# Parameter steps handed out at 1.0 a tile step, S5 input tiles mixed among the RWKV pairs' tiles, and three scratch pools moved

## The chip, the cores and the metric

The kernel runs on one core of a Trainium2 chip. Its time is the device time of one execution in microseconds (us). Three runs of the kernel before gave 2048.62, 2050.24 and 2052.57 us, so its median is 2050.24 us. A lower time is better.

## The reference, cut to what matters

The reference is one layer of a diffusion backbone for 256 latent tokens with 256 context tokens ahead of them. The part around the change is the token mixer:

```python
p = einsum('btd,dn->btn', h, w_in)              # one projection feeds both mixers
q = p[..., :RWKV_IN]; u = p[..., RWKV_IN:]      # RWKV-7 part, S5 part
# RWKV-7: 16 heads x 64, two directions, a scan of matrix states over the tokens
s = s * w_t - (s @ kk_t) b_t + v_t k_t;  y = s @ r_t
# S5: 64 groups x 16 channels, 64 complex states a group, two directions
lam, bb = zoh(a, log_step, b)                   # depends on weights alone
bu = bb @ u;  state = scan(lam, bu);  y5 = c @ state
o = concat([norm(y) * gate, glu(gelu(y5 + d*u))]);  x = x + gt * (o @ w_out)
```

Behind it stands a gated feed-forward part, whose weights are most of what the kernel reads. The modulation vectors (shift, scale and gate of each sub-layer) are products of silu(c) with a weight of 2048 x 12288.

## The kernel before

**Stages.** The projection runs in tiles of 128 output columns, each with 16 blocks of 128 rows as fp32r matmuls (three a block, line L430). A *pair* is two RWKV heads: three tiles (k, v, r), then a preparation of some 36 steps (`prep`, `factors`, `products`) that writes the pair's factors to HBM (`own`). After every second pair a triangular solve (`solve`, mostly POOL) gives a block `pt`. The chains (`chain`, four in all, run two at a time by `chains(0)` and `chains(1)`) then walk over eight chunks each, and load `own` and `pt` back. S5 needs its input `u` from eight tiles of its own (`s5_projected`), and it needs tables that depend on weights alone.

**Parameter steps.** These tables and some modulation blocks are made in a generator of 84 steps, called `mods` here: `early` (20 steps, five modulation blocks, L374 and L379), `s5_factors` (32 steps, tiles `MP`, `mt`, `MB`, L1319 to L1328) and `s5_toeplitz` (32 steps, tiles `C`, `mck`, `MCk`, `ks`, L1170 to L1204). The three follow one another. In `s5_toeplitz` the tiles have one buffer each: the next `C` is loaded when the last one's readers are done, and the next `MCk` is written when the last one has left for HBM.

**Who hands out the order.** `beside` walks over the tiles' steps. To each tile step it adds two or three steps of `prepare`, and 0.72 steps of `mods` on average. When `prepare` ends, `switch` closes the pools of that phase, opens those of the chains, and goes on with `chains(0)` (two steps to a tile step). Counting the generators' steps from the code: `mods` is handed out to its end at tile step 117, the switch comes at step 123, and at that point six of the eight S5 tiles are still to come. After the tiles, `s5` and `rwkv` (rest of `chains(0)`, then `chains(1)` with the outputs of the first two, `post`) are woven step by step, with seven more modulation blocks (`late`) at every twelfth step, from the pool `mw`.

**How an order becomes queues.** A planner makes one queue for each engine and one for SP, which issues all DMAs. It simulates the program, and of the instructions that are ready in its simulation it takes the one handed out earliest. (`urgent` with an offset puts a generator far ahead; with offset 0, as for `prepare` and `chains`, its instructions count as handed out at the same place as the tile step beside them.) An instruction is ready when its inputs are there and its tile has a free buffer. Each engine then runs its queue strictly in that order.

**Room.** Scratch pools are two stacks, one from the left end of each partition's memory and one from the right end. A pool opened in the room of a closed one waits for that one's last user. From the tile sizes in the code, in bytes of a partition: left: constants 19,040, `pp` (scratch of `early` and `s5_factors`) 12,288, `rp` (of the preparation) 59,392; after the switch `yp` 4,096 and `rl0` (of `chains(0)`) 65,536, so that `rl0` ends at 88,672; later `mp` (of `post`) 14,336 and `rl1` (of `chains(1)`) 65,536, so that `rl1` ends at 103,008. Right: `hp` (the projection's input) 65,536, `wp` (its weights, and `u`) 15,360, `rs` (of the solves) 29,696, `tp` (of `s5_factors`' and `s5_toeplitz`' tables) 8,704, so that `tp` lies from 110,592 to 119,296 from the right end. All four stay open until the tiles and `mods` are done; then come `mw` 12,288, `ul` 8,192, `U2` and `Z` 49,408, `sc` 7,168, `si` 16,384. PSUM has a right pool `w`=2, `d`=1 banks (tiles; `mods`), which is closed before S5's `s`=2, `d`=1 opens.

Of the kernel before, what the change touches and what calls it, by code (L numbers as in the profile page):

```python
# [10 lines left out]
F32 = mybir.dt.float32  # L11
# [7 lines left out]
NP, NF = 8, 44  # L19
# [106 lines left out]
def run(gen):  # L126

    while True:
        try:
            next(gen)  # L130
        except StopIteration as e:
            return e.value


def chained(gens):
    for g in gens:
        yield from g


def woven(a, b, na, nb):  # L140

    ia = ib = 0
    left = [a, b]
    while left:
        g = left[0] if len(left) == 1 else (a if ia * nb <= ib * na else b)
        if next(g, left) is left:
            left.remove(g)
            continue
        if g is a:
            ia += 1  # L150
        else:
            ib += 1
        yield


class Body:
# [834 lines left out]
            yield  # L991
        yield from fill

    def beside(self, tiles, prep, mods, switch, rates=(5, 9), every=0.72):


        n, rate = 0, rates[0]
        for stage in tiles:
            n += 1
            for _ in range(rate // 2 + n % 2 * (rate % 2)):  # L1000
                if next(prep, self) is self:
                    prep, mods, rate = switch(mods)
            for _ in range(int(n * every) - int((n - 1) * every)):
                next(mods, None)
        return mods
# [348 lines left out]
    def s5_scan(self, pool, half):  # L1354

        V = self.nc.vector if half else self.nc.gpsimd
        gs = slice(16 * half, 16 * half + 16)
        Z = self.Z[:, :, :, gs]
        A, I = self.AR[:, 0, :, :, gs], self.AI[:, 0, :, :, gs]
        pair = lambda n: Z[:, 1 + n:129 - n:127 - 2 * n]  # L1360
        for n in range(32, 63):
            a = pool.tile([128, 2, 2, 16], F32, tag="sa%d" % half, name="sa")
            b = pool.tile([128, 2, 2, 16], F32, tag="sb%d" % half, name="sb")
            V.tensor_tensor(out=a, in0=pair(n - 1), in1=A, op=ALU.mult)
            V.tensor_tensor(out=b, in0=pair(n - 1)[:, :, ::-1], in1=I, op=ALU.mult)
            V.tensor_tensor(out=a, in0=a, in1=pair(n), op=ALU.add)
            V.tensor_tensor(out=pair(n), in0=a, in1=b, op=ALU.add)
            if n % 2:
                yield
# [205 lines left out]
def body(tc, A, out):  # L1575
    with ExitStack() as ctx:
        b = Body(ctx, tc, A, out)
        nc = tc.nc
        b.gelu = None
        b.od, b.Y, b.q, b.ud, b.last, b.done, b.os = {}, {}, {}, {}, None, 0, None  # L1580
        b.uld = tc.dram_tile([8, 128, 256], F32, name="uld")
        left, right = (lambda st, name, bufs=1: st.enter_context(tc.tile_pool(name=name, bufs=bufs, side="left")),
                       lambda st, name, bufs=1: st.enter_context(tc.tile_pool(name=name, bufs=bufs, side="right")))

        hx, lx, mx, sx, sb, p0, pl, pr, pm, wx, ex = (ExitStack() for _ in range(11))
        b.lx = lx
        hp = right(hx, "hp")
        b.wp = right(hx, "wp", 2)
        b.pp = left(ex, "pp", 6)
        p0.enter_context(b.psum("left", t=5, v=1, m=1, y=1))  # L1590
        first = [(0, 0), (1, 0), (3, 0), (4, 0), (5, 256)]
        parts = [(6, 2), (7, 2), (9, 2), (10, 2), (12, 2), (13, 2)]
        b.parts = {}
        with tc.tile_pool(name="sp0", bufs=1, side="left") as sp0:
            ps = b.start(hp, [(i, lo, "t") for i, lo in first], parts, lambda: b.s5_params(sp0))
        b.rp = left(lx, "rp")
        b.lora(*ps[0:2])
        for (p, j), x in zip(((0, 0), (0, 1), (0, 2)), ps[2:]):
            run(b.projected(p, j, x))
        p0.close()  # L1600

        pr.enter_context(b.psum("right", w=2, d=1))
        pl.enter_context(b.psum("left", l=1, g=2, m=2))
        b.rs = right(hx, "rs")
        tiles = []
        for p in range(1, NP):
            tiles += [b.projected(p, j) for j in range(3)]
        tiles.append(b.gates())
        tiles += [b.s5_projected(jj, b.wp) for jj in range(8)]
        tp = right(hx, "tp")  # L1610
        early = chained(b.mod_steps(blk, 4 * blk, b.pp, "d", 1, "d", 6, "pp") for blk in range(8, 13))
        prep = b.urgent(b.prepare(), 0)
        first = []

        def switch(mods):
            run(early)
            lx.close()
            ex.close()
            pl.close()
            pm.enter_context(b.psum("left", m=1))  # L1620
            pl.enter_context(b.psum("left", c=2, y=2))
            b.yp = left(mx, "yp")
            first.append(b.chains(0))
            return first[0], woven(b.urgent(b.solving), mods, 44, 16), 4

        rest = b.beside(chained(tiles), prep, chained([early, b.s5_factors(b.pp, tp), b.s5_toeplitz(tp)]), switch)
        run(rest)
        hx.close()
        pr.close()

        pr.enter_context(b.psum("right", s=2, d=1))
        mw = right(wx, "mw")
        spu, spb = right(sx, "spu"), right(sb, "spb")
        with tc.high_priority(100000):
            b.s5_begin(spb, spu)
        late = chained(b.mod_steps(blk, 4 * blk, mw, "d", 2, "d", 3) for blk in range(13, 20))
        run(b.paced(woven(b.rwkv(first[0], lx, mx, pl), b.s5(sx, sb), 140, 100), late, 12))
        wx.close()

        b.x = right(ctx, "xp").tile([128, 16, 256], F32, name="x")  # L1640
        fw = right(ctx, "fw", 2)
        with tc.tile_pool(name="om", bufs=2, side="right") as om:
            b.ffn_scales(om)
            run(b.mixed(om, fw, b.x, b.x1, 0, b.os))
            for st in (lx, mx, pl, pm, pr):
                st.close()
            ctx.enter_context(b.psum("left", w=4, m=3, d=1))
            b.ffn_input(left(ctx, "h2p"), om, fw)

        b.ffn(left(ctx, "fp"), fw, chained(b.mod_steps(blk, 4 * blk, fw, "d", 2, "d", 2) for blk in range(20, 24)))  # L1650
# [15 lines left out]
```

## Time and profile before

| | us |
|---|---|
| median of three runs | 2050.24 |
| the profiled execution's own time | 2047.77 |
| its span, first to last instruction | 2046.0 |
| PE busy (TensorE matmul) | 1857.8 (91%) |
| DVE busy (VectorE) | 1272.2 (62%) |
| ACT busy (ScalarE) | 894.4 (44%) |
| POOL busy (GpSimd) | 336.9 (16%) |

All times of rows are counted from the span's start. Busy time is the time in which at least one instruction of the engine ran; a busy PE is not PE at its peak, since its matmuls overlap and their ends are modelled. PEclk is the granted TensorE clock as a share of 2.4 GHz. In a timeline, the bracket at a line's end tells how long the engine had been idle before it, and what it then waited for.

### The profile page before, as it was taken

How to read it: one execution, taken by the hardware profiler on the slowest of the kernel's cores; microseconds unless marked ns; L12 is line 12 of the kernel's file. 1: busy time of each engine (PE TensorE's matmuls, PEld its weight loads, DVE VectorE, ACT ScalarE, POOL GpSimd, SP SyncE). 2: the span in 40 equal slices, each digit the busy share in tenths (PEclk: the TensorE clock that was granted, in tenths of full speed). 3: DMA queues.
4: the chain of work that ended last, by engine and by line, in shares of the span. 5: the costliest groups of instructions: out<-in, count | busy, mean ns of one | idle time of the engine just before them, and what ended most of it. 6: DMA issues, size and time to landing. Idle time of an engine off the chain costs nothing.

```text
span 2046.0 us, 35653 instructions
## 1 busy us (share of the span) xinstructions
PE 1857.8 (91%) x13704; PEld 1446.0 (71%) x13704; DVE 1272.2 (62%) x2400; ACT 894.4 (44%) x1617; POOL 336.9 (16%) x517
## 2 busy tenths in 40 slices
PE   3899989999989799746899989999999999999997
PEld 1557766677867668524566667888888888888886
DVE  7525877559799465443865667766666566645544
ACT  2234654435646534212223444555555455544442
POOL 0300034074183471121800000000000000000000
PEclk8899988778889899857799999999999999999998
DMA  8882576525435867839879764566666665566664
GB/s 322 306 304 91 185 249 232 200 86 174 135 112 175 257 206 233 283 117 308 299 269 338 266 214 156 193 220 216 222 214 223 224 207 183 183 186 185 186 188 136
DMA packets 181147, 433.80 MB, mean 212 GB/s; under 512 B 27248, under 2 KB 59376, under 8 KB 178160
## 3 DMA queue, kind: packets, MB, share of 16 engines
q1 hardware_dynamic: 180976, 431.52, 63.5%
q8 instruction: 108, 1.77, 0.4%
q14 instruction: 63, 0.52, 0.1%
HBM read 373.12 MB, written 62.52 MB: 213 GB/s over the span
## 4 chain that ended last, share of the span: by engine, by line
PE 53%; DMA 6%; DVE 4%; POOL 2%; issue 1%; ACT 1%; SPq 0%; DVEq 0%; ACTq 0%; POOLq 0%
PE ps_w L230 28%; PE ps_m L230 12%; PE ps_w L430 3%; PE ps_d L379 2%; DMA modw<-modw_in 2%; PE ps_s L230 1%; DMA mcd<-MCk 1%; PE ps_c L841 1%; PE ps_s L1404 1%; DMA own<-own 1%; DMA MB<-mbd 1%; DMA C<-s5c_in 1%; PE ps_d L1195 1%; POOL tmp L716 0%; POOL TM L718 0%
## 5 line engine op out<-in xcount | busy, mean ns | idle before, releaser
L220 DVE TENSOR_TENSOR lo<-raw,hi 128x1024 fp32r<-128x1024 f32 (+1 forms) x327 | 371.1, 1136 | 239.0 <-ACT hi L219 235.1
L219 ACT ACTIVATE hi<-raw 128x1024 fp32r<-128x1024 f32 (+1 forms) x327 | 322.3, 987 | 285.2 <-PE ps_w L230 207.9
L230 PE MATMUL ps_m<-h,hi 128*128 128x512 f32 x688 | 247.2, 398 | 2.3 <-ACT hi L219 2.3
L230 PE MATMUL ps_w<-h,hi 128*128 128x512 f32 x688 | 248.7, 400 | 0.6 <-DVE h L1516 0.6
L230 PE MATMUL ps_w<-hid,hi 128*128 128x512 f32 x704 | 247.6, 398 | 0.0
L230 PE MATMUL ps_w<-hid,lo 128*128 128x256 f32 x704 | 195.1, 281 | 0.0
L230 PE MATMUL ps_m<-h,lo 128*128 128x256 f32 x688 | 187.2, 282 | 1.2 <-DVE lo L220 1.2
L230 PE MATMUL ps_w<-h,lo 128*128 128x256 f32 x688 | 186.5, 281 | 0.3 <-DVE lo L220 0.3
L430 PE MATMUL ps_w<-hhi,lo 128*128 128x512 f32 (+2 forms) x448 | 174.8, 390 | 7.8 <-DVE lo L214 7.8
L430 PE MATMUL ps_w<-hhi,hi 128*128 128x512 f32 (+2 forms) x448 | 175.1, 391 | 1.1 <-ACT hi L213 1.1
L430 PE MATMUL ps_w<-hlo,hi 128*128 128x512 f32 (+2 forms) x448 | 171.2, 382 | 0.0
L214 DVE TENSOR_TENSOR lo<-raw,hi 128x512 fp32r<-128x512 f32 (+1 forms) x144 | 110.0, 767 | 97.4 <-ACT hi L213 94.8
L213 ACT ACTIVATE hi<-raw 128x512 fp32r<-128x512 f32 (+1 forms) x144 | 88.9, 620 | 181.4 <-PE ps_w L430 68.3
L230 PEld LDWEIGHTS ps_w<-h,hi 128*128 128x128 f32 x688 | 129.2, 188 | 41.2 <-ACT up L238 10.9
L230 PEld LDWEIGHTS ps_w<-hid,hi 128*128 128x128 f32 x704 | 131.3, 188 | 31.4
L230 PEld LDWEIGHTS ps_m<-h,hi 128*128 128x128 f32 x688 | 129.4, 188 | 30.3 <-ACT hi L219 3.0
L230 PEld LDWEIGHTS ps_w<-hid,lo 128*128 128x128 f32 x704 | 133.0, 189 | 1.5
L230 PEld LDWEIGHTS ps_m<-h,lo 128*128 128x128 f32 x688 | 129.9, 189 | 5.6 <-DVE lo L220 1.8
L230 PEld LDWEIGHTS ps_w<-h,lo 128*128 128x128 f32 x688 | 129.9, 189 | 3.6 <-DVE lo L220 0.7
L430 PEld LDWEIGHTS ps_w<-hhi,lo 128*128 128x128 f32 (+1 forms) x448 | 91.0, 203 | 34.5 <-DVE lo L214 15.1
L430 PEld LDWEIGHTS ps_w<-hhi,hi 128*128 128x128 f32 (+1 forms) x448 | 91.3, 204 | 26.4 <-ACT hi L213 6.8
L430 PEld LDWEIGHTS ps_w<-hlo,hi 128*128 128x128 f32 (+1 forms) x448 | 91.7, 205 | 15.4 <-issue 3.1
(387 smaller groups left out, 3464.2 us busy)
## 6 DMA issues: line engine op xcount, KB each, us to landing
raw<-wup_in SPq DMA_DIRECT2D x176, 512.0 KB
modw<-modw_in SPq DMA_DIRECT2D x152, 512.0 KB
raw<-wdn_in SPq DMA_DIRECT2D x80, 512.0 KB
raw<-win_in SPq DMA_DIRECT2D x140, 256.0 KB
own<-own SPq DMA_DIRECT2D x32, 1024.0 KB
modw<-modw_in SPq DMA_DIRECT2D x80, 256.0 KB
own<-own SPq DMA_DIRECT2D x32, 640.0 KB
raw<-wout_in SPq DMA_DIRECT2D x38, 256.0 KB
```

Source lines behind the costliest of these rows:

```text
L213: nc.scalar.activation(out=hi, in_=raw, func=AF.Copy)
L214: nc.vector.tensor_tensor(out=lo, in0=raw, in1=hi.bitcast(F32), op=ALU.subtract)
L219: nc.scalar.activation(out=hi, in_=src, func=AF.Copy)
L220: nc.vector.tensor_tensor(out=lo, in0=src, in1=hi.bitcast(F32), op=ALU.subtract)
L230: mm = self.nc.tensor.matmul(out, lhsT=a, rhs=b, start=(n == 0), stop=(n == last), skip_group_check=True)
L379: self.behind(nc.tensor.matmul(ps[32 * j:32 * j + 32, :], lhsT=self.silu[:, k], rhs=ws[j], start=(k < 4), stop=(k >= 12)))
L430: self.nc.tensor.matmul(out, lhsT=w[:, j], rhs=x[:, k, lo:T], start=(k == 4 * job["qs"][0] and n == 0), stop=(k == 4 * job["qs"][1] - 1 an ...
L841: nc.tensor.matmul(U[q:q + 64, i], lhsT=pt[q:q + 64, :, 8 * i + n], rhs=Ws[q:q + 64, i], start=True, stop=True)
L1195: nc.tensor.matmul(ps[32 * g:32 * g + 32, o:o + 128], lhsT=Bd[:, 2 * g + d, i].rearrange("p a h -> p (a h)"), rhs=m, start=(i == 0 and d = ...
L1404: nc.tensor.matmul(outs[q], lhsT=X, rhs=m[:, ::-1] if d else m, start=False, stop=(d == 1 and i == 1))
```

## The change

`beside` hands out 1.0 steps of `mods` to a tile step in place of 0.72. By the same count `mods` is then handed out to its end at tile step 84, and the switch comes at step 123 as before. Each pair's three tiles are followed by one S5 tile, the eighth S5 tile and the gates' tile come last, and no tile is left at the switch. `tp` is closed at the switch, after all of `mods` has been handed out; `hp`, `wp` and `rs` are closed after the tiles as before. `mw` is opened at the switch, on the left, under `yp` and `rl0`, so that `rl0` ends at 35,424 + 65,536 = 100,960 and `rl1` at 115,296. On the right, `ul` is then first, and `ul`, `U2`, `Z`, `sc` and `si` end at 80,128, inside the 80,896 of `hp` and `wp`; two scratch tiles of `s5_scan` get one buffer in place of two for this.

```diff
-    def beside(self, tiles, prep, mods, switch, rates=(5, 9), every=0.72):
+    def beside(self, tiles, prep, mods, switch, rates=(5, 9), every=1.0):
...
-            a = pool.tile([128, 2, 2, 16], F32, tag="sa%d" % half, name="sa")
-            b = pool.tile([128, 2, 2, 16], F32, tag="sb%d" % half, name="sb")
+            a = pool.tile([128, 2, 2, 16], F32, tag="sa%d" % half, name="sa", bufs=1)
+            b = pool.tile([128, 2, 2, 16], F32, tag="sb%d" % half, name="sb", bufs=1)
...
         for p in range(1, NP):
-            tiles += [b.projected(p, j) for j in range(3)]
-        tiles.append(b.gates())
-        tiles += [b.s5_projected(jj, b.wp) for jj in range(8)]
-        tp = right(hx, "tp")
+            tiles += [b.projected(p, j) for j in range(3)] + [b.s5_projected(p - 1, b.wp)]
+        tiles += [b.s5_projected(NP - 1, b.wp), b.gates()]
+        tp = right(tx, "tp")
...
         def switch(mods):
-            run(early)
-            lx.close()
-            ex.close()
-            pl.close()
+            run(mods)
+            for st in (tx, lx, ex, pl):
+                st.close()
             pm.enter_context(b.psum("left", m=1))
             pl.enter_context(b.psum("left", c=2, y=2))
+            wide.append(left(wx, "mw"))
             b.yp = left(mx, "yp")
             first.append(b.chains(0))
-            return first[0], woven(b.urgent(b.solving), mods, 44, 16), 4
+            return first[0], b.urgent(b.solving), 4
...
-        mw = right(wx, "mw")
+        mw = wide[0]
...
-        wx.close()
...
-            for st in (lx, mx, pl, pm, pr):
+            for st in (lx, mx, wx, pl, pm, pr):
                 st.close()
```

## Rows read from the trace of the kernel before

**Rows 1.** The page: busy tenths, granted clock and DMA share in 40 slices.
```profile
PE   3899989999989799746899989999999999999997
DVE  7525877559799465443865667766666566645544
POOL 0300034074183471121800000000000000000000
PEclk8899988778889899857799999999999999999998
DMA  8882576525435867839879764566666665566664
```

**Rows 2.** Windows by stage: span, busy PE, PEld, DVE, ACT, POOL, clock, DMA.
```profile
205.00:690.00 485.00, 452.86 (x3431) 343.27 (x3430) 372.35 (x664) 260.02 (x553) 178.83 (x241) 0.86 0.52 176
690.00:852.00 162.00, 146.26 (x1763) 115.48 (x1761) 86.52 (x154) 62.91 (x143) 72.31 (x88) 0.93 0.75 238
852.00:941.00 89.00, 38.21 (x338) 24.24 (x338) 27.60 (x56) 11.22 (x28) 16.40 (x14) 0.62 0.60 186
941.00:1054.00 113.00, 97.62 (x1536) 72.73 (x1535) 81.08 (x275) 32.36 (x84) 51.69 (x136) 0.86 0.84 292
1054.00:1254.00 200.00, 188.60 (x1426) 132.63 (x1426) 128.08 (x266) 84.65 (x146) 0.00 (x0) 0.96 0.74 263
1254.00:2046.00 792.00, 774.03 (x4400) 657.35 (x4400) 467.39 (x650) 377.55 (x544) 0.00 (x0) 0.99 0.62 196
```

**Rows 3.** Tiles MP and MCk: the table steps' DVE instructions, first and last start.
```profile
L1319 DVE TENSOR_TENSOR MP<-bs,Ls x32: 664/684/1598, 397.1 to 670.6; 128x512 f32<-128x512 f32 x32
...
L1181 DVE TENSOR_TENSOR MCk<-C,Ls x32: 718/759/1769, 676.4 to 913.2; 128x576 f32<-128x576 f32 x32
```

**Rows 4.** Windows of tile MCk: busy PE (8 instructions a step), PEld, DVE, then clock.
```profile
676.00:745.00 69.00, 6.51 (x72) 3.71 (x72) 16.61 (x18) 0.90 0.75 232
745.00:852.00 107.00, 9.32 (x104) 5.06 (x104) 20.01 (x26) 0.95 0.73 240
852.00:917.00 65.00, 10.84 (x80) 5.73 (x80) 16.31 (x20) 0.59 0.50 169
```

**Rows 5.** Waits in 852 to 917: us in total, times, longest.
```profile
POOL mck L1182 <- DMA C<-s5c_in: 40.1, 4, 21.1
...
DVE MCk L1181 <- DMA mcd<-MCk: 16.7, 7, 5.5
```

**Rows 6.** Timeline of POOL: three steps of the tables, and the chains' first instructions.
```profile
886.56 1.21 POOL L1182 TENSOR_TENSOR mck<-C,Ls 128x576 f32<-128x576 f32 x1 [6.34 <-DVE rs_a L201]
889.64 1.21 POOL L1182 TENSOR_TENSOR mck<-C,Ls 128x576 f32<-128x576 f32 x1 [1.87 <-DVE MCk L1184]
895.20 1.21 POOL L1182 TENSOR_TENSOR mck<-C,Ls 128x576 f32<-128x576 f32 x1 [4.35 <-DMA C<-s5c_in]
...
689.98 2.83 POOL L796 MEMSET PT<- 32x1024 f32 x3 [9.63 <-ACT hi L213]
...
919.33 3.94 POOL L796 MEMSET PT<- 32x1024 f32 x4 [7.11 <-DMA kd<-ks]
```

**Rows 7.** Timeline of DVE and of PE: the second chains' and S5's first instructions.
```profile
919.26 0.27 DVE L821 MEMSET ZE<- 64x256 f32 x1 [4.47 <-DMA kd<-ks]
...
914.84 1.07 PE L1195 MATMUL ps_d<-MCk,s5Bd 128*32 128x128 f32 x8 [2.69 <-DVE MCk L1187]
916.47 0.83 PE L1345 MATMUL ps_s<-U,MB 128*64 128x64 f32 x10 [0.56 <-issue]
```

**Rows 8.** Timeline of ACT: the chains' first Ws, last ZE, and one chunk.
```profile
710.81 0.38 ACT L836 ACTIVATE Ws<-ps_c 128x256 f32<-128x256 f32 x1 [1.01 <-PE ps_c L832]
...
941.31 0.38 ACT L836 ACTIVATE Ws<-ps_c 128x256 f32<-128x256 f32 x1 [1.20 <-PE ps_c L832]
...
1054.00 0.38 ACT L843 ACTIVATE ZE<-ps_c 64x256 f32<-64x256 f32 x1 [1.47 <-PE ps_c L841]
...
837.98 0.66 ACT L836 ACTIVATE Ws<-ps_c 128x256 f32<-128x256 f32 x2 [0.85 <-PE ps_c L832]
...
845.02 0.38 ACT L836 ACTIVATE Ws<-ps_c 128x256 f32<-128x256 f32 x1 [4.04 <-PE ps_c L832]
```

**Rows 9.** Windows of line L430, then of L214: the tiles' PE and DVE after 690.
```profile
690.00:836.00 146.00, 74.87 (x281) 53.41 (x279) 0.92 0.73 229
...
690.00:836.00 146.00, 19.26 (x23) 0.92 0.73 229
```

**Rows 10.** Windows of line L379 (late modulation), then of L1404 (S5 outputs), after the chains.
```profile
1054.00:1254.00 200.00, 26.05 (x144) 3.62 (x144) 0.96 0.74 263
...
1054.00:1254.00 200.00, 15.52 (x390) 11.47 (x390) 0.96 0.74 263
```

**Rows 11.** Tile U: S5's output matmuls, first and last start.
```profile
L1395 PE MATMUL ps_s<-TZ,U x128: 272/297/423, 1014.6 to 1113.4; 128*32 128x128 f32 x128
```

**Rows 12.** Costliest groups, `s5_scan` on POOL: busy, mean ns, idle before.
```profile
L1365 POOL TENSOR_TENSOR sb<-Z,s5pw 128x64 f32<-128x64 f32 x31 | 11.5, 369 | 0.0
```

More of the change, by code (lines that the diff above doesn't have):

```diff
@@ L1583, in body @@
                        lambda st, name, bufs=1: st.enter_context(tc.tile_pool(name=name, bufs=bufs, side="right")))
-        hx, lx, mx, sx, sb, p0, pl, pr, pm, wx, ex = (ExitStack() for _ in range(11))
+        hx, lx, mx, sx, sb, p0, pl, pr, pm, wx, ex, tx = (ExitStack() for _ in range(12))
         b.lx = lx
@@ L1606, in body @@
         for p in range(1, NP):
-            tiles += [b.projected(p, j) for j in range(3)]
-        tiles.append(b.gates())
-        tiles += [b.s5_projected(jj, b.wp) for jj in range(8)]
-        tp = right(hx, "tp")
+            tiles += [b.projected(p, j) for j in range(3)] + [b.s5_projected(p - 1, b.wp)]
+        tiles += [b.s5_projected(NP - 1, b.wp), b.gates()]
+        tp = right(tx, "tp")
         early = chained(b.mod_steps(blk, 4 * blk, b.pp, "d", 1, "d", 6, "pp") for blk in range(8, 13))
         prep = b.urgent(b.prepare(), 0)
-        first = []
+        first, wide = [], []
         def switch(mods):
-            run(early)
-            lx.close()
-            ex.close()
-            pl.close()
+            run(mods)
+            for st in (tx, lx, ex, pl):
+                st.close()
             pm.enter_context(b.psum("left", m=1))
             pl.enter_context(b.psum("left", c=2, y=2))
+            wide.append(left(wx, "mw"))
             b.yp = left(mx, "yp")
             first.append(b.chains(0))
-            return first[0], woven(b.urgent(b.solving), mods, 44, 16), 4
+            return first[0], b.urgent(b.solving), 4
         rest = b.beside(chained(tiles), prep, chained([early, b.s5_factors(b.pp, tp), b.s5_toeplitz(tp)]), switch)
```

## The prediction

> **What bounds the kernel now.** I read the page's slices first, then the busy time by stage, then single lines around the gap that these show. In the slices PE is full from two thirds of the way to the end, and has its deepest hole in slices 17 to 20, where the clock falls too [rows 1]. By stage [rows 2]: tiles and preparation (205 to 690) have PE busy for 453 of 485 us; the rest of the tiles beside the first two chains 146 of 162; then 852 to 941, where PE is busy for 38 of 89 us at a clock of 0.62; the last two chains beside S5, 98 of 113; the mixer's end, 189 of 200; the feed-forward part, 774 of 792. Behind 1254 nothing but PE counts, and the change leaves it alone. So the question is when the stretch that ends at 1254 ends.
>
> What fills the hole is the last parameter part, `s5_toeplitz`. Its DVE instructions run from 676.4 to 913.9, right behind those of `s5_factors`, 397.1 to 670.6 [rows 3]. In 852 to 917 it has the machine nearly to itself and still needs 65 us for ten steps (80 PE instructions, 8 a step) [rows 4], as each step waits for its own single buffers: POOL 40 us for the next `C`, DVE 17 us for `MCk` to have left [rows 5].
>
> Two things wait for its end. S5's first matmul stands at 916.47, directly behind its last ones; the PSUM pool that S5 needs is the one whose bank it uses [rows 7]. And `chains(1)` begins there: POOL's clearing of `PT` at 919.33 was released by the DMA kd<-ks, the last reader of `tp`, and so was DVE's of `ZE` at 919.26 [rows 6, 7]. The chains' arithmetic has nothing to do with `ks`; what they share is room. `rl1` ends at 103,008 bytes from the left and waited; `rl0` ends at 88,672, and its clearing ran at 690, in the middle of `s5_toeplitz` [rows 6]. So `tp` begins somewhere between these two, and who reaches into it waits for all of it: two engines' first instructions waited, on tiles that lie apart.
>
> **The change, part by part.**
>
> *The rate.* It alters when a step is handed out, not when it is ready. Before, all 84 steps were handed out by tile step 117, ahead of the switch at 123, which the trace has at 690 (the first clearing for `chains(0)` [rows 6]). Yet of the last 32 steps 23 ran after 745 [rows 4]. They are late against their place, and the planner takes the earliest handed out that is ready, so they were not passed over: they waited for inputs and buffers of their own. Handing them out at step 84 makes old steps older. I give it 0 us; what it could gain if the order were what holds them is the first rival.
>
> *S5 tiles among the pairs.* Six tiles move from behind the switch to before it. They are 75 us of PE and 19 us of DVE there [rows 9]. If DVE set the pace up to the switch (372 of 485 us) it moves by 19 us, if PE did (453 of 485) by 75 [rows 2]; PE is the fuller, but part of its busy time is at a clock of 0.86. I take 50: the preparation ends at 740. Their six writes of `u` and six of `ul` go to SP's queue with them; nothing waits for those before S5.
>
> *The end of the parameter steps, M.* I keep their start, 676. To 740 they go as from 676 to 745: 9 steps in 69 us, 7.7 each, so 8.3 steps [rows 4]. 23.7 are left. The stretch 852 to 917 gives 6.5 a step; it holds one wait of 21 us for a `C` [rows 5]. The fastest pair of steps there, POOL 886.56 to 895.20, gives 4.3 [rows 6]. Halfway between them 5.4: 23.7 x 5.4 = 128, so M = 868 (842 and 894 by the two ends). So they end some 50 us sooner than now (917), since tiles and chains are out of the way.
>
> *Room.* `rl0` now ends at 100,960, 12,288 more than before, which is 86% of the way from the end that didn't wait to the one that did, and the diff closes `tp` just ahead of it. So `chains(0)` waits for the last DMA out of `tp`, at M, in place of 690. Queued behind these first instructions are the chains' own loads on SP, `states` on ACT, and every later chain, `post` and mixer step.
>
> The Trainium skill settles the room in a way that the trace alone does not: "SBUF — State Buffer", section "SBUF size: 192, 224, or 256?", leaves about 208 KiB of a partition to use, 212,992 bytes. By that, `rl0` and `tp` need 100,960 + 119,296 = 220,256 and overlap, where before 207,968 fitted; the trace agrees on the side it shows, `rl0` not waiting before and `rl1` waiting.
>
> *The chain of the end.* Clearing to the first Ws takes 21 us (689.98 to 710.81) or 22 (919.33 to 941.31) [rows 6, 8]; I use 21. Two chains beside S5's first half took 941.31 to 1054.00 = 113 [rows 8]; the same company meets `chains(0)` now. `chains(1)` then has its 21, and meets only S5's outputs and `post`. The fastest chunk of the trace took 837.98 to 845.02 = 7.0 us [rows 8], eight of them 56, which bounds it from below; from above 113. I take 93, nearer to the row with the same company. Chains end at 868 + 21 + 113 + 21 + 93 = 1116, against 1054.
>
> *From there to 1254.* Now 200 us, PE full. S5 starts at M, 48 us sooner than at 916; its outputs, last at 1113 now [rows 11], end at 1065, before the chains do: 15.5 us less. Of the 18 late modulation steps in it (144 instructions, 26 us) ten more have been handed out before, as the woven part is now longer by the steps of `chains(0)`: 14.5 us less [rows 10]. 200 - 30 = 170, bounds 155 and 200. End of the stretch: 1116 + 170 = 1286, against 1254: 32 us later.
>
> *The rest.* One buffer in `s5_scan` in place of two: both tiles are written and read by one engine in its own order, 0 us; if each of 31 rounds waited as long as one of its instructions on POOL (0.37 us), 11 us, beside the chains [rows 12]. `mw` on the left, S5's pools inside `hp` and `wp`: S5's loads may start at 740 in place of 844, but its first matmul needs the PSUM bank that `s5_toeplitz` holds until M, so no more than M's 50 us is gained there, and that is hidden behind the chains. S5 no longer needs the room of `rs`; the last solve was done long before 917, so 0.
>
> Sum, against the profiled execution: span 2046.0 + 32 = 2078. The median of the runs shown lies 4.2 above that span, so I predict 2050.2 + 32 = **2082 us**. In one line: the end is M + 418, and M decides at 836.
>
> **The rivals.**
>
> *The steps do speed up (faster).* If order, not their own buffers, holds the steps back, the higher rate brings M near the switch. For it: 84 steps at the fastest pace of 4.3 us [rows 6] are 361 us, and 205 to 740 has room for them; in 397 to 670 the `s5_factors` steps took 8.5 us each with DVE crowded [rows 2, 3]. Against: the stretch at 852, where nothing crowds them and they are hardly faster. With M = 800 the end is at 1218, 36 us sooner: 2014 us. Chance 0.19.
>
> *`chains(0)` doesn't wait.* If room is given tile by tile, or `rl0` ends short of `tp`, `chains(0)` runs from 740 to about 890 beside the steps, these go at 6.5 (M = 894), and S5 and `chains(1)` start 23 us sooner than now (917): 2027 us. Against it stand the two engines that waited for all of `tp` [rows 6, 7]. Chance 0.06.
>
> *The steps get slower.* More tiles delay their first part (the S5 tile of pair 1 stands before the tiles that free `pp`, 75 / 6 = 12 us), and a queue of SP that stalls once more costs 20 or more, as the 21 us did [rows 5]. M = 920 or above: 2134 us and later. This decides from M = 900. Chance 0.09.
>
> *The forecast*, the chains held by the room of the steps: 0.66. This case alone spans 2048 to 2118.
>
> **How the numbers follow.** A change under 0.2% (4 us) can't be told from none here. The forecast's 0.66 is 0.57 slower, 0.05 the same and 0.04 faster, as M would have to be 32 us sooner than taken to break even, under its lower bound of 842, and only the chains or the mixer's end can help. The first rival gives 0.17 faster and 0.02 the same, the second 0.05 and 0.01, the third 0.09 slower. So faster 0.26, the same 0.08, slower 0.66. The range 2015 to 2130 leaves out half of the first rival and half of the third.
>
> **What would show it.** In the changed kernel's trace: no L430 instruction behind the switch; the steps of `MCk` running on beyond the last tile with PE nearly empty and the clock low; POOL's first clearing of `PT` released by kd<-ks, at 840 to 900 and not near 740; S5's first matmul at the same time; the stretch from there to the mixer's end about 418 us. I am wrong if `MCk` ends before the last tile (the steps did speed up), or if the first `PT` is cleared while `MCk` still runs (room is not shared).

## The result, and the profile after

The changed kernel takes 2183.14 us (median of 4 runs, 2179.72 to 2185.21) against 2051.4 for the kernel before: 1.064 times as long, 95% interval [1.0619, 1.0663]. The forecast was 2082: slower was right, but by 132 us and not by 32. The profiled execution has a span of 2183.1.

The page of the changed kernel, in the 40 slices of [rows 1]:

```profile
PE   4899998998989813369989999999999999999997
...
POOL 0200043073183272252000100000000000000000
PEclk8899998999999855576678999999999999999998
```

The hole is deeper, and behind it the clock stays at 6 to 7 for three slices in which PE is full (19 to 21, counted from 1). The windows by stage, columns as in [rows 2]: up to the start of the last solve, up to the end of the table steps, the wait for the first chunk, the first two chains, the wait between, the last two chains, the mixer's rest, the feed-forward part.

```profile
205.00:740.00 535.00, 491.63 (x3469) 363.74 (x3467) 389.14 (x676) 274.27 (x572) 185.50 (x243) 0.93 0.54 178
740.00:905.00 165.00, 54.84 (x812) 39.03 (x811) 56.76 (x72) 31.07 (x71) 71.55 (x91) 0.55 0.41 136
905.00:933.00 28.00, 12.58 (x225) 11.77 (x224) 1.09 (x4) 5.99 (x16) 3.67 (x4) 0.56 0.85 241
933.00:1102.00 169.00, 148.12 (x1620) 101.86 (x1617) 84.58 (x287) 32.01 (x82) 43.95 (x124) 0.69 0.58 200
1102.00:1131.00 29.00, 23.26 (x250) 14.67 (x250) 5.75 (x23) 4.96 (x13) 3.78 (x4) 0.62 0.79 227
1131.00:1252.00 121.00, 116.94 (x1360) 81.01 (x1360) 51.92 (x120) 40.22 (x85) 10.66 (x12) 0.87 0.70 241
1252.00:1390.00 138.00, 130.35 (x764) 98.89 (x762) 109.17 (x232) 65.25 (x117) 0.00 (x0) 1.00 0.69 234
1390.00:2183.00 793.00, 775.17 (x4400) 658.45 (x4400) 467.33 (x650) 377.56 (x544) 0.00 (x0) 0.99 0.62 196
```

The last row is the 792 of [rows 2] again, so everything lies ahead of it: the stretch that ended at 1254 ends at 1390. PE waits from 740 to 905 (55 of 165 us busy). Then 933 to 1102 is something else: PE is busy for 148 of 169 us, at a clock of 0.69, on two chains for which [rows 2] has 98 of 113 us at 0.86.

The wait is the one that was forecast. POOL's and PE's timelines in the changed kernel, beside [rows 6, 7]: the first `PT` for each pair of chains, the last product of the table steps, and S5's first.

```profile
908.30 3.72 POOL L796 MEMSET PT<- 32x1024 f32 x4 [6.94 <-DMA kd<-ks]
...
1107.16 3.95 POOL L796 MEMSET PT<- 32x1024 f32 x4 [107.75 <-PE ps_y L877]
...
903.98 1.07 PE L1195 MATMUL ps_d<-MCk,s5Bd 128*32 128x128 f32 x8 [2.69 <-DVE MCk L1187]
905.57 2.71 PE L1345 MATMUL ps_s<-U,MB 128*64 128x64 f32 x45 [0.51 <-ACT ks L1202]
```

`chains(0)` is let go by kd<-ks, where before `chains(1)` was. The table steps themselves, against [rows 3]: `MP`'s DVE group.

```profile
L1319 DVE TENSOR_TENSOR MP<-bs,Ls x32: 670/692/1607, 447.1 to 693.3; 128x512 f32<-128x512 f32 x32
```

And against [rows 4], windows of `MCk` (PE, eight instructions a step, PEld, DVE, clock).

```profile
698.00:740.00 42.00, 1.90 (x25) 1.09 (x25) 6.01 (x8) 0.92 0.64 211
740.00:850.00 110.00, 18.25 (x144) 9.86 (x144) 28.88 (x34) 0.57 0.45 150
850.00:905.00 55.00, 11.70 (x88) 6.53 (x88) 17.98 (x22) 0.50 0.32 108
```

`s5_factors` starts 50 us later than in [rows 3] and ends 23 later; by 740 four steps of `s5_toeplitz` have been started, and the other 28 take 165 us.

### The profile page after: what moved, and what is told of

The parts are those of the page before. It is cut to its first block, busy times and chain, and to the rows that moved or that the text cites. A ratio compares the mean times of both kernels' runs of the same rounds, so it can differ in the third digit from the quotient of the medians.

```text
span 2183.1 us, 35662 instructions
## 1 busy us (share of the span) xinstructions
PE 1913.8 (88%) x13704; PEld 1470.4 (67%) x13704; DVE 1274.7 (58%) x2400; ACT 897.1 (41%) x1617; POOL 336.4 (15%) x517
## 4 chain that ended last, share of the span: by engine, by line
PE 58%; DMA 11%; DVE 9%; issue 2%; ACT 2%; POOL 2%; SPq 1%; DVEq 0%; ACTq 0%; POOLq 0%
PE ps_w L230 25%; PE ps_m L230 11%; PE ps_w L430 4%; DMA mcd<-MCk 3%; PE ps_d L379 3%; PE ps_c L841 2%; DMA raw<-wout_in 2%; PE ps_s L1404 1%; DMA MB<-mbd 1%; PE ps_s L230 1%; PE ps_g L663 1%; DMA kd<-ks 1%; DVE lo L214 1%; DMA modw<-modw_in 1%; DVE MCk L1181 1%
## 5 line engine op out<-in xcount | busy, mean ns | idle before, releaser
L230 PE MATMUL ps_m<-h,hi 128*128 128x512 f32 x688 | 248.2, 399 | 2.0 <-ACT hi L219 2.0
L230 PE MATMUL ps_w<-h,hi 128*128 128x512 f32 x688 | 248.6, 400 | 0.8 <-DVE h L1516 0.8
L230 PE MATMUL ps_w<-hid,hi 128*128 128x512 f32 x704 | 247.6, 398 | 0.0
L230 PE MATMUL ps_w<-hid,lo 128*128 128x256 f32 x704 | 195.1, 281 | 0.0
L230 PE MATMUL ps_m<-h,lo 128*128 128x256 f32 x688 | 187.9, 283 | 1.1 <-DVE lo L220 1.1
L230 PE MATMUL ps_w<-h,lo 128*128 128x256 f32 x688 | 186.5, 281 | 0.3 <-DVE lo L220 0.3
L430 PE MATMUL ps_w<-hhi,lo 128*128 128x512 f32 (+2 forms) x448 | 173.1, 387 | 10.7 <-DVE lo L214 10.6
L430 PE MATMUL ps_w<-hhi,hi 128*128 128x512 f32 (+2 forms) x448 | 174.4, 389 | 8.4 <-ACT hi L213 8.4
L214 DVE TENSOR_TENSOR lo<-raw,hi 128x512 fp32r<-128x512 f32 (+1 forms) x144 | 110.7, 772 | 120.2 <-ACT hi L213 110.8
L430 PE MATMUL ps_w<-hlo,hi 128*128 128x512 f32 (+2 forms) x448 | 167.7, 374 | 0.0
L230 PEld LDWEIGHTS ps_w<-h,hi 128*128 128x128 f32 x688 | 129.2, 188 | 41.2 <-ACT up L238 10.9
L230 PEld LDWEIGHTS ps_w<-hid,hi 128*128 128x128 f32 x704 | 131.3, 188 | 31.4
L230 PEld LDWEIGHTS ps_m<-h,hi 128*128 128x128 f32 x688 | 130.0, 189 | 30.2 <-ACT hi L219 2.8
L230 PEld LDWEIGHTS ps_m<-h,lo 128*128 128x128 f32 x688 | 130.6, 190 | 5.6 <-DVE lo L220 1.8
L230 PEld LDWEIGHTS ps_w<-hid,lo 128*128 128x128 f32 x704 | 133.0, 189 | 1.5
L230 PEld LDWEIGHTS ps_w<-h,lo 128*128 128x128 f32 x688 | 129.9, 189 | 3.6 <-DVE lo L220 0.7
L1195 PE MATMUL ps_d<-MCk,s5Bd 128*32 128x128 f32 x256 | 31.9, 394 | 107.9 <-DVE MCk L1187 70.6
L430 PEld LDWEIGHTS ps_w<-hhi,lo 128*128 128x128 f32 (+1 forms) x448 | 87.9, 196 | 45.6 <-DVE lo L214 21.9
L430 PEld LDWEIGHTS ps_w<-hhi,hi 128*128 128x128 f32 (+1 forms) x448 | 88.4, 197 | 37.4 <-ACT hi L213 15.6
```

What stands on the lines that cost most here:

```text
L214: nc.vector.tensor_tensor(out=lo, in0=raw, in1=hi.bitcast(F32), op=ALU.subtract)
L230: mm = self.nc.tensor.matmul(out, lhsT=a, rhs=b, start=(n == 0), stop=(n == last), skip_group_check=True)
L430: self.nc.tensor.matmul(out, lhsT=w[:, j], rhs=x[:, k, lo:T], start=(k == 4 * job["qs"][0] and n == 0), stop=(k == 4 * job["qs"][1] - 1 an ...
L1195: nc.tensor.matmul(ps[32 * g:32 * g + 32, o:o + 128], lhsT=Bd[:, 2 * g + d, i].rearrange("p a h -> p (a h)"), rhs=m, start=(i == 0 and d = ...
```

## The experiments

The table has for each run the median time; M, the end of the last table step; the first clearing of `PT`; the first Ws to the last ZE of `chains(0)` and of `chains(1)`, each with its length; and the mixer's end, all from its profiled execution. Ws and ZE are two tiles that ACT writes in every chunk of a chain. "Changes" counts, from first Ws to last ZE, neighbouring matmuls of PE of which one is of the chains' own kind with 64 rows (L841, L872) and the other is not, with the time from start to start of all of them, in us. S5's L1404 has 64 rows too, but is counted with the others; put beside L841 and L872, it would make 189 changes in 51 us of the 165 in 42, and 59 in 23 us of e9's 57 in 19. (Some expectations count S5's rows as a class of their own: 198 and 89 there are 165 and 78 here. For whole programs they count in the order as built.)

```
run                        time   M   PT   chains(0)      changes  chains(1)      changes  mixer's end
before                   2051.4  916  690   711- 849 139   38  9    941-1054 113   78 25   1254
after                    2183.1  905  908   933-1102 169  165 42   1131-1252 121   84 21   1390
e1 all but the room      2074.6  939  746   779- 888 109   64 22    965-1095 130   84 27   1275
e2 room only             2134.7  886  889   914-1028 114   79 24   1054-1188 134   98 20   1336
e3 tile order only       2087.0  954  765   798- 907 108   82 21    979-1111 132   94 29   1297
e4 rate only             2075.4  918  696   716- 852 136   36 10    945-1076 131  126 35   1280
e5 after, PE kept busy   2187.2  899  905   932-1103 171  165 44   1133-1249 116   84 21   1386
e6 before, PE kept busy  2084.9  929  697   718- 857 139   38 11    964-1081 118   98 30   1293
e7 after, two buffers    2101.8  847  851   874-1019 145  120 31   1046-1169 123   66 18   1305
e8 before, two buffers   2042.6  845  689   714- 862 147   50 13    906-1039 133   71 24   1241
e9 after, held           2126.9  906  909   933-1055 122   57 19   1080-1191 111   43 11   1337
e10 before, held         2068.0  919  693   714- 848 134   33  8    945-1079 135   53 15   1284
e11 before, two, held    1999.7  855  695   720- 853 133   38 11    874- 995 121   41 16   1211
e12 rate, held           2068.2  914  699   720- 854 134   35 10    940-1074 134   53 15   1277
e13 all but room, held   2068.3  939  750   783- 886 103   31 20    966-1075 109   37 15   1276
e14 room only, held      2114.2  882  885   911-1023 112   33 14   1058-1166 108   45 16   1323
e15 e13, two buffers     2037.4  882  757   789- 900 110   40 16    931-1050 120   51 13   1239
e16 after, two, held     2098.3  858  862   884-1013 128   57 19   1049-1169 120   53 26   1311
```

### One part undone, one part alone: e1 to e4

e1 undoes the room in the changed kernel:

```
-            wide.append(left(wx, "mw"))
...
-        mw = wide[0]
+        mw = right(wx, "mw")
...
```

> The changed kernel with one thing undone: mw is opened on the right again, behind the end of tp, so that rl0 lies where it lay before and shares no room with tp. Rate, tile order, sa/sb and the early closing stay. Theory 'room' (the loss is chains(0) waiting for the last table step): PT is cleared near 745 while MCk still runs, chains(0) is over by about 900, the table steps end at 900 to 920, S5 and chains(1) start there as in the kernel before (917), and the time is 2030 to 2065. Rival 'order' (the loss comes from the S5 tiles among the pairs' tiles and from the steps' order): PT is cleared early, yet the time stays above 2110. Rival 'clock' (the chains are slow because PE was idle from 760 to 904): PE isn't idle here, so this run can't part it from 'room'.

e2 does the room alone in the kernel before:

```
-        tp = right(hx, "tp")
+        tp = right(tx, "tp")
...
-            run(early)
-            lx.close()
+            run(mods)
+            for st in (tx, lx, ex, pl):
+                st.close()
...
+            wide.append(left(wx, "mw"))
...
```

> The kernel before with one part of the change alone: mw is opened on the left under yp and rl0, and tp is closed ahead of them, with what that needs (all steps are issued ahead of the switch). Rate 0.72, the six S5 tiles behind the switch and two buffers of sa and sb stay. Theory 'room': PT of chains(0) is cleared by the release of kd<-ks; without chains beside them the steps end near 890; the end follows 487 us behind that, as in the changed kernel (904 to 1391), and 792 of the feed-forward part behind it: 2140 to 2190. Rival 'order': the time is within 15 us of the kernel before, 2036 to 2066.

e3 has the tile order alone, e4 the rate alone:

```
-            tiles += [b.projected(p, j) for j in range(3)]
-        tiles.append(b.gates())
-        tiles += [b.s5_projected(jj, b.wp) for jj in range(8)]
+            tiles += [b.projected(p, j) for j in range(3)] + [b.s5_projected(p - 1, b.wp)]
+        tiles += [b.s5_projected(NP - 1, b.wp), b.gates()]
```

```
-    def beside(self, tiles, prep, mods, switch, rates=(5, 9), every=0.72):
+    def beside(self, tiles, prep, mods, switch, rates=(5, 9), every=1.0):
```

> The kernel before with the tile order of the change alone: one S5 tile behind the three of each pair, the gates last. Theory 'room': the switch moves some 55 us later (690 to about 745), chains(0) then runs beside the table steps and is over near 900, the steps end within 20 us of 917, and the time is within 20 us of the kernel before: 2031 to 2071. Rival 'order': 2100 and more.

> The kernel before with the rate 1.0 in place of 0.72 alone. Theory 'the steps wait for inputs and for their own single buffers': nothing moves by more than 4 us, 2047 to 2055, and MCk starts and ends within 5 us of where it did (676 and 914). Rival 'the order of handing out holds them': MCk ends before 880 and the time falls by 20 us or more, to below 2030.

Ratios: e1 1.0104 [1.0058, 1.0151], e2 1.0405 [1.0361, 1.0448], e3 1.0170 [1.0134, 1.0206], e4 1.0110 [1.0066, 1.0154]. The first clearings of `PT` in e1 and in e2, from POOL's timeline:

```profile
746.46 3.87 POOL L796 MEMSET PT<- 32x1024 f32 x4
```

```profile
888.76 3.72 POOL L796 MEMSET PT<- 32x1024 f32 x4 [6.93 <-DMA kd<-ks]
```

With `rl0` back in its place `chains(0)` starts at 746 and runs beside the steps; the room given up makes it wait for them in the other kernel too. The room is the largest part: 109 us on top of the rest (2183.1 - 2074.6), 83 alone. But none of the four lies in its expected range: e1 is 10, e3 16 and e4 20 us above it, e2 5 below. e4 is the plainest. Its table steps stand where they stood [rows 3]:

```profile
L1181 DVE TENSOR_TENSOR MCk<-C,Ls x32: 716/758/1773, 677.8 to 915.5; 128x576 f32<-128x576 f32 x32
```

so the rate did nothing to them, and yet the end is 26 us later, 24 of it behind M. It is lost while PE is busy: in the stretch of `chains(1)` it does 1563 matmuls in 122 us, where [rows 2] has 1536 in 98.

```profile
945.00:1076.00 131.00, 121.77 (x1563) 87.00 (x1564) 81.41 (x275) 33.19 (x85) 51.14 (x136) 0.78 0.75 266
```

Nor do the costs add: the tile order and the rate cost 35 and 24 us alone, but e1, which has both, costs 23. e3 also has M 38 us later, where 20 were allowed: with the tile order alone `s5_factors` starts at 452 already, as in the changed kernel.

### Clock or order: e5, e6

Eight matmuls behind each of the last 24 (e5) or 8 (e6) table steps, so that PE isn't idle:

```
+                    for _ in range(8 if e >= 2 else 0):
+                        nc.tensor.matmul(ps[:, 256:512], lhsT=self.con[:, 0:128], rhs=self.con[:, 0:256],
+                                         start=True, stop=True, skip_group_check=True)
```

> The changed kernel with eight matmuls (128x256, constants, into the unused half of the step's own PSUM bank) behind each of the last 24 table steps; nothing reads what they write. They keep TensorE at work from 762 to 904, where it was busy for 30% at a granted clock of 0.50. Theory 'clock' (the two chains take 169 and 121 us in place of 113 and 93 because PE comes to them at a low clock and stays there): the clock is 0.9 or more in 800 to 904, chains(0) takes 115 to 140 from its first Ws to its last ZE, and the time falls to 2130 to 2160. Rival 'order' (what stands between the chains' instructions in PE's queue, S5's outputs and the modulation): chains(0) still takes 160 or more and the time is 2170 to 2195.

> The kernel before with the same eight matmuls behind each of the last eight table steps (some 865 to 917, clock 0.59 there). Theory 'clock': the stretch 917 to 1054, at 0.86, goes at 0.95 and the time falls by 5 to 15 us, to 2036 to 2046. Rival 'order': the time stays within 6 us, or rises by 10 to 30 because the new instructions move the planner's order, as the rate alone did.

e5's windows:

```profile
800.00:850.00 50.00, 47.58 (x479) 38.38 (x478) 16.78 (x19) 11.47 (x23) 11.80 (x13) 0.99 0.38 123
850.00:904.00 54.00, 45.33 (x281) 35.68 (x283) 15.86 (x20) 4.28 (x13) 10.91 (x9) 0.97 0.27 90
904.00:930.00 26.00, 9.46 (x195) 8.63 (x193) 2.25 (x6) 5.71 (x14) 3.67 (x4) 0.68 0.91 240
960.00:980.00 20.00, 17.15 (x200) 10.55 (x192) 19.38 (x67) 4.35 (x12) 17.94 (x53) 0.55 0.75 266
1000.00:1020.00 20.00, 20.00 (x132) 12.82 (x130) 10.78 (x53) 1.97 (x5) 0.00 (x0) 0.50 0.19 56
```

The clock was up, 0.99 and 0.97 where the changed kernel has 0.50 (with PE busy for 34 of 142 us from 762 to 904, so 24% and not the 30% that the expectation names), and it changed nothing: the time is 2187.2 us (1.0657 [1.0593, 1.0721]), `chains(0)` takes 171 us, with the same 165 changes, and the clock is down to 0.50 again at 1000, with PE busy all the time. In the wait (904 to 930) it had fallen too, but the first 18 us of `chains(0)` are at 0.95, against 0.80 for the first 17 in the changed kernel. A cold start isn't the cause. e6 was slower (1.0158 [1.0115, 1.0202]), above both of its ranges: M came 13 us later, `chains(0)` ended 8 later. Its stretch of chains beside S5 took 118 us in place of 113, at a changed order, so it says little on the clock.

What PE does at 1000 to 1020 is seen in its timeline in the changed kernel:

```profile
1011.86 0.48 PE L841 MATMUL ps_c<-Ws,PT 64*64 64x64 f32 x2
1012.27 0.47 PE L850 MATMUL ps_c<-ZE,own 128*64 128x64 f32 x2
1012.68 0.48 PE L841 MATMUL ps_c<-Ws,PT 64*64 64x64 f32 x2
...
1017.56 0.48 PE L841 MATMUL ps_c<-Ws,PT 64*64 64x64 f32 x2
```

One chain's `U` step (64 rows) and the other's `Sp` step (128 rows) stand in PE's queue two by two: 30 matmuls in 6.1 us, 0.20 each. PE counts as busy, and moves little. The 128-row matmuls by themselves follow right behind in the same trace; ten start between these two rows, 0.05 us each:

```profile
1018.12 0.31 PE L851 MATMUL ps_c<-ZO,own 128*64 128x64 f32 x1
...
1018.66 0.63 PE L877 MATMUL ps_y<-own,ZO 128*64 128x64 f32 x4
```

The same `U` steps one behind the other, in e9 (L847 there is L841, L1410 is L1404):

```profile
1009.35 2.05 PE L847 MATMUL ps_c<-Ws,PT 64*64 64x64 f32 x32
1011.33 1.31 PE L1410 MATMUL ps_s<-MC,Z 64*32 64x128 f32 x34
```

32 in 2.0 us, 0.06 each. The clock has no part in this factor of 3.3, as the windows of the alternating matmuls in the changed kernel and of these 32 in e9 show (their counts hold those that reach in from outside); it is 0.50 in both:

```profile
1011.00:1018.00 7.00, 7.00 (x38) 4.74 (x38) 1.43 (x8) 0.00 (x0) 0.00 (x0) 0.50 0.45 150
...
1009.35:1011.33 1.98, 1.98 (x36) 1.86 (x32) 1.81 (x12) 0.38 (x1) 0.00 (x0) 0.50 0.48 86
```

"TensorEngine Tiling (Array Packing)" of the Trainium skill, section "Key Properties", says that a change of tiling mode drains the engine; these rows agree. By them a change cost some 0.3 us, an estimate: 6.1 us less 30 x 0.06, over 15 changes.

### The steps sped up: e7, e8

```
-                C = pool.tile([128, 4, 2, 16], F32, tag="C", name="C", bufs=1)
+                C = pool.tile([128, 4, 2, 16], F32, tag="C", name="C", bufs=2)
...
-                    MC = pool.tile(sh, F32, tag="MC", name="MCk", bufs=1)
+                    MC = pool.tile(sh, F32, tag="MC", name="MCk", bufs=2)
```

> The changed kernel with two buffers each for C and MCk in the table steps, so that a step needn't wait until the one before has left. Theory 'room, end = M + constant': the steps take about 4 us each in place of 5.9 from 762 on, they end at 850 to 875 in place of 904, PT of chains(0) is cleared 4 us behind that, and the time falls by as much as M does: 2130 to 2160. Rival 'order': M falls but the time doesn't follow, 2170 or more.

> The kernel before with two buffers each for C and MCk (rl0 keeps its own room). Theory 'S5 and chains(1) start at the later of M and the end of chains(0)': the steps end at 870 to 890 in place of 917, and the time falls by 25 to 45 us, to 2005 to 2028. Rival 'order': M falls but what follows takes longer, and the time is within 10 us of before or above.

M falls by 58 and by 71 us, so the steps did wait for their own single buffers. e7 (1.0248 [1.0202, 1.0293]) gains 81, more than M and 28 more than its range, with 120 changes in `chains(0)` in place of 165. e8 (0.9955 [0.9932, 0.9979]) gains 9, far less: `chains(0)` now ends at 862, behind M, the first chunk of `chains(1)` comes 41 us behind the clearing (22 before), and `chains(1)` takes 133 us. Neither time follows M one for one.

### The order held: e9 to e12

A group of matmuls that one step of a chain issues may start on PE only behind the group issued before it:

```
         for n, a in enumerate(group):
...
+            for b in (self.block if block else ()):
+                self.tc.add_manual_dep(a, b, mybir.DependencyInfo(mybir.DependencyClass.NoSync,
+                                                                  mybir.DependencyReason.DATA), reason="block")
+        if block:
+            self.block = [a.name for a in group]
```

The planner orders PE's queue so, and no semaphore is added. e9 is this on the changed kernel, e10 on the kernel before, e11 on e8 and e12 on e4.

> The changed kernel with the chains' matmuls held together: each group of eight or so that one step of a chain issues may start on PE only behind the group that the chains issued before it (an order without a semaphore). No work is added. Theory 'order' (in the changed kernel chains(0) takes 169 us because PE changes 198 times between matmuls with 64 and with 128 rows, 54 us at some 0.27 each, where chains(1) of the kernel before changes 89 times for 27 us): the program now has 199 such changes from the first to the last chain matmul in place of 333; at 0.2 us each the time falls by some 27 us, to 2145 to 2165, and chains(0) to 130 to 150. Rival 'the held-back steps wait': a chain step whose inputs are ready waits behind the other chain's; the time is 2178 or more. M stays within 8 us of 904.

> The kernel before with its chains' matmuls held together in the same way. It has 112 changes of row shape in place of 130. Theory 'order': 4 us less by 0.2 us each, within 8 us: 2039 to 2055. Rival 'the held-back steps wait': 2060 or more.

> The kernel before with two buffers each for C and MCk (2042.6 alone) and with its chains' matmuls held together: 84 changes of row shape in place of 140. Theory 'order': 56 x 0.2 = 11 us less than 2042.6: 2022 to 2038. Rival 'the held-back steps wait': 2045 or more.

> The kernel before with the rate 1.0 (2075.4 alone) and with its chains' matmuls held together: 114 changes of row shape in place of 178, and 112 with the rate 0.72. Theory 'order' (the rate itself costs nothing, but moves the planner's order, and the 24 us lie in it): most of the 24 us go, and the time is within 8 us of the kernel before with held-together chains at the rate 0.72. Rival 'the rate itself costs': it stays 18 us or more above that.

e9 (1.0375 [1.0337, 1.0414]) is 56 us faster than the changed kernel with the same work and the same M, twice the 27 that the changes alone were to bring and 18 below its range. Its chains and the wait between them:

```profile
933.00:1056.00 123.00, 100.55 (x1460) 69.40 (x1456) 81.71 (x288) 29.62 (x79) 43.69 (x124) 0.81 0.72 247
1056.00:1080.00 24.00, 16.38 (x232) 11.30 (x230) 4.80 (x21) 3.15 (x8) 3.79 (x4) 0.78 0.87 234
1080.00:1192.00 112.00, 109.57 (x1510) 76.02 (x1506) 52.51 (x119) 42.24 (x91) 9.43 (x12) 0.99 0.85 300
```

`chains(0)` takes 122 us and not 169. The changes, waits in them included, take 23 us less (42 to 19); the rest isn't assigned. Other things moved with them: the clock rises from 0.69 to 0.81, and 130 of S5's output matmuls (L1395, L1404) stand among the chains' in place of 262. e10 missed its range and came out as its rival had it: 17 us slower (1.0090 [1.0059, 1.0121]), though it has fewer changes (53 for 78 in `chains(1)`, which yet takes 135 us in place of 113):

```profile
945.00:1079.00 134.00, 106.34 (x1544) 72.57 (x1546) 79.89 (x275) 31.28 (x83) 51.82 (x136) 0.81 0.73 252
```

So the count alone doesn't set the time. PE is idle for 28 us there, against 15 in [rows 2], which fits held steps that wait; what they wait for was not tested. e12 (1.0073 [1.0046, 1.0100]) is equal to e10, 2068.2 and 2068.0: at a held order the rate costs nothing, within some 6 us by the intervals.

e11 is faster than both kernels: 1999.7 us, 0.9760 [0.9727, 0.9793], 22 us below its expected range. Its two parts alone don't tell it, as e8 gains 9 us and e10 loses 17. M is 855, just behind the end of `chains(0)` (853), and `chains(1)` has its first chunk at 874 in place of 941. In its windows (the rest of tiles and first chains, the wait, the last chains) the hole of [rows 2] is gone:

```profile
690.00:855.00 165.00, 146.29 (x1797) 112.93 (x1792) 110.85 (x174) 69.02 (x156) 87.42 (x97) 0.89 0.78 248
855.00:874.00 19.00, 14.85 (x93) 11.90 (x93) 5.39 (x20) 4.01 (x9) 3.80 (x4) 0.93 0.84 203
874.00:995.00 121.00, 97.97 (x1601) 73.78 (x1597) 67.67 (x187) 36.28 (x93) 49.40 (x127) 0.81 0.96 342
```

### The parts at a held order: e13 to e16

No new edit: e13 is e1 held, e14 is e2 held, e15 is e13 with the two buffers of e7, e16 is e9 with them.

> The changed kernel with mw on the right again (rl0 shares no room with tp) and the chains' matmuls held together: all of the change but the room, at a held order (97 changes of row shape). Theory 'room and order' (the room costs the wait of chains(0), everything else only moved the order): 2058 to 2080, like the kernel before with held-together chains at either rate (2068), so that the room is worth 2127 - 2068 = some 59 us. Rival 'the tile order costs by itself' (35 us alone in e3): 2095 or more.

> The kernel before with the room given up (as e2) and the chains' matmuls held together. Theory 'room and order': the room alone costs the same 50 to 70 us on 2068: 2110 to 2140, with M near 885 and chains(0) starting there. Rival 'the room costs only through the order': 2090 or less.

> e13 with two buffers each for C and MCk, beside e11 (1999.7): does the S5 tiles' place among the pairs' tiles, which leaves nothing to do behind the switch but chains and steps, gain anything once order and steps are mended? Theory 'room and order': M falls to some 850 and with it the start of S5, 2000 to 2030 (171 changes of row shape against 84 in e11, 17 us at 0.2). Rival 'the tile order gains': below 1996. Rival 'the tile order costs': above 2035.

> The changed kernel with two buffers each for C and MCk and with its chains' matmuls held together. Theory 'end = M + constant' at a held order: M falls from 903 to some 846 as in e7, and the time by as much, 2127 to 2055 to 2085; even so it is above the kernel before, as M would have to be near 835. Rival 'order': the time falls by less than 25 us, 2102 or more.

e13 (1.0078 [1.0052, 1.0105]) is 2068.3, the same as e10 and e12. So at a held order rate, tile order, single buffers and pools together cost nothing that can be told from noise, though the switch is 57 us later and M 20. The room costs 59 us on top of them (2126.9 - 2068.3) and 46 alone (e14, 1.0304 [1.0275, 1.0334], against e10). e15 (0.9930 [0.9904, 0.9956]) is 38 above e11 and 7 above its range, as the rival 'the tile order costs' had it: with the steps sped up the later switch costs, since `chains(0)` now ends at 900, behind M (882), and is what `chains(1)` waits for. e16 (1.0229 [1.0195, 1.0262]) was missed by 13: M falls by 48 and the time by 29.

## Why the prediction was wrong

The 132 us are, by the medians: 17 from the kernel before to the same kernel held (e10), 0 for all but the room (e13), 59 for the room (e9), and 56 from the held order to the one that the planner made of the change. This is one way to divide them; at the planner's own orders everything but the room is 23 (e1), and the room with the order that came with it 109. The prediction had a term for the room and none for the order. Of the 101 us between the forecast and the result, M is 37 and the chain behind M 67 (3 too many, as the median lay 4 us above the profiled span before, and on it here). The span of the forecast's own case, 2048 to 2118, isn't added up from its bounds, which give 2004 to 2158; these don't hold 2183 either.

**What bounds the kernel**: right. All of it lies ahead of the feed-forward part, and S5 still waits for M; `chains(0)` now does so in the place of `chains(1)`, which waits for `chains(0)`.

**The rate, 0**: right for the last 32 steps, which stand in e4 where they stood, and for the time at a held order (e12). Wrong as a cost: alone it takes 24 us, since another time of handing out gives PE another order behind M.

**S5 tiles, preparation over at 740**: right; the last preparation matmul in PE is at 741, and e1 clears `PT` at 746. The tiles themselves ended 18 us behind it, at 759.

**M, 868**: 37 too early, and outside 842 to 894. I kept 676 as the start, and it was 698, since `s5_factors` began 50 us later, as it does with the tile order alone (452 in e3); that delay I had only as a rival, priced at 12. Four steps and not 8.3 were started by 740, and the others took 5.9 us each, not 5.4: 28 x 5.9 = 165 for 128.

**Room**: right, down to the releasing DMA (908.30). "SBUF — State Buffer" of the Trainium skill, section "SBUF size: 192, 224, or 256?", by which `rl0` and `tp` couldn't both fit, agrees with it.

**The chain of the end**: this is the term that failed. Forecast and measured, from M on: to the first Ws 21 and 28; `chains(0)` 113 and 169; between them 21 and 29; `chains(1)` 93 and 121; the tail 170 and 138: 418 and 485. A stretch's duration was carried to another place as if it hung on the work alone. "The same company meets chains(0) now" held with the room alone: 114 us (e2), and 112 held (e14), as I said. In the changed kernel the chains' same instructions, mixed in another way, took 169. `chains(1)` was too cheap in any order (108 at best, e14), and S5's outputs, forecast to end at 1065, ran to 1172 between the chains' matmuls:

```profile
L1395 PE MATMUL ps_s<-TZ,U x128: 272/297/423, 982.1 to 1172.1; 128*32 128x128 f32 x128
```

The tail is shorter than forecast in part because 64 of the mixer's 640 output matmuls (L230) had run ahead of it too; with 576 they are 15 us less than in [rows 2]'s stretch, 109 for 124. At a held order "M + 418" is M + 431 (e9) and M + 441 (e14), which breaks even at M = 823 and 813; the earliest M of any of these kernels was 845.

**M decides one for one**: not so. 58 us of M gave 81 (e7) at the planner's order and 48 gave 29 (e16) at a held one.

**The rivals.** That the steps speed up didn't happen, and e7 and e8 show why: their own single buffers, as the prediction read from [rows 5]. That `chains(0)` doesn't wait is e1's case, made by moving the room back; there the time is 2074.6, and not the 2027 of that rival. "The steps get slower" came true in part, M being behind 900; by M + 418 it gives 905 + 418 + 792 + 4 = 2119, still 64 short. None of them had PE busy and slow.

That the order costs is shown by holding it (e9, e12, e13), and that alternating shapes are slow by the rows above. What stays open is how much of the 56 us is the alternation, why the held order costs the kernel before 17 us, and why the granted clock falls to 0.50 in stretches in which PE is never idle; that the changes of row shape bring it about is only argued, from e9 and e5.

## What to carry to other kernels

A full engine isn't an engine at its pace: read how many instructions it does in a busy stretch, and in what order shapes follow each other, before a stage's duration is carried to another place. Where a planner writes the order, a part tried alone also tries another order; hold the order first, then price the part, and give the range a term for it (17 to 56 us here). Before moving a long chain of steps, look at its own buffers: two tiles with a second buffer each, with the chains held together, gave 2.4%; at a held order the change without its room gave nothing, and its room lost 59 us.

## What the runs showed of the hardware

- Matmuls of 64 rows and of 128 rows that alternate two by two took 0.20 us each (changed kernel, 1011.86 to 1017.97), and those of one shape in a row 0.06 (64 rows, e9) and 0.05 (128 rows, changed kernel), all at a granted clock of 0.50.
- PE busy for 20.0 of 20 us had a granted clock of 0.50 (e5, 1000 to 1020), 96 us after a stretch at 0.97. Being busy by the profile didn't keep the clock up here.
